# A bidirectional DeltaNet scan: state product on quarters, operands two steps ahead, a written order of two engines

## The chip, the cores and the metric

The kernel runs as one program on one core of a Trainium2 chip. The core has TensorE (PE, matmuls), VectorE (DVE), ScalarE (ACT), GpSimd (POOL) and SyncE (SP, which issues DMAs); each works through its own list of instructions in order, and semaphores hold an instruction until its inputs are there. The metric is the time of one execution on the device, in microseconds.

## The reference, cut to what matters

One layer of an encoder on 1024 tokens of width 1024: conditioning, a combined projection, two mixers side by side (attention and a gated DeltaNet), their gated merge, and a mixture of 16 experts. The DeltaNet runs forward and backward over 16 chunks of 64 tokens, 8 heads, 64 x 64 state each:

```python
T = triangular_solve(eye + L, eye)            # one 64x64 inverse per chunk, head, direction
def step(state, inp):
    u_n, w_n, a_n, qg_n, kd_n, gl_n = inp
    v_new = u_n - w_n @ state
    o_n = qg_n @ state + a_n @ v_new
    state = state * gl_n[..., None, None] + jnp.einsum('bhck,bhcv->bhkv', kd_n, v_new)
    return state, o_n
o = (o_fwd + o_bwd)
o = rmsnorm(o, dn_norm_w) * silu(dz)
mod = silu(c) @ W_ada + b_ada                  # six rows of 1024: the conditioning
```

The kernel computes all this in 32-bit floating point; a projection is three matmuls on high and low parts of its operands (hTh and hTl of the activations, wh and wl of the weights).

## The kernel before, in words

The stages follow each other: normalisation and the DeltaNet's projections with their short convolution (`dn_group`, to 210 us); decays and chunk products, two chunks at a time (`dn_tile`, to about 287); the inverse of 32 x 32 blocks on VectorE (`dn_invert`, lines 512 to 546, to 368.7), while TensorE does the attention's projections and the first gates (L285); the scan (`scan`, 399 to 707); attention, merge, output projection and experts.

The scan takes forward chunk t and backward chunk 15 - t in one step. Two chunks of 64 rows share the 128 partitions. `scan_load` brings a step's operands from DRAM on SP's queue. `scan_merge` makes the off-diagonal block of the two inverses from 32 x 32 blocks: VectorE transposes (L607), 16 small matmuls (L610), ScalarE, 16 more (L617), ScalarE. `scan_step` multiplies k and q by the state (L632): the state stands in `St` as block-diagonal 128 x 128 pairs of heads, which ScalarE copies anew from `Sc` each step (L665). Half of each product is the part for `X` = u - k state (L635, L639), the other half is the query's part of the output (L675 to L678). Then v_new (L644, L649, L650), the state's update (L654, L659, L662) and the output (L669).

Between these stand `fills`: matmuls of later projections (`late_fill`, L1154), each 128 x 512, 48 to a group; constants `FILL` say how many are asked for at which point of a step. In steps 0 to 7 `attn_prep` readies the attention's q, k and v for 128 tokens (transposes L149, VectorE L744 to L771), in later ones `scan_post` normalises finished output rows. `mods` works out the conditioning, a multiply-add on VectorE per 128 x 512 weight tile (L909), five groups of eight tiles before the scan, three in it; its sums go through a cast on ScalarE (L895), a difference on POOL (L896) and two matmuls (L898).

The order of instructions on each engine is set by a scheduler from the program's order and its own estimates, except within the inverse's columns, where VectorE's order is written down. Loads of the inverse's input run on POOL's queue.

```python
w = self.W[t % 2]                              # two sets of operands, loaded one step ahead
nc.tensor.matmul(pk[:, 2 * p:2 * p + 2, :].rearrange("p h c -> p (h c)"), kq[d][:, p],
                 self.St[:, d, p, :], start=True, stop=True, skip_group_check=True)   # L632
FILL = 12, 10, 8, 8, 48                        # per step 12 + 10 + 8 + 8, before the scan 48
```

## Time and profile before

| what | us |
|---|---|
| median of 3 runs | 1733.75 |
| lowest and highest | 1732.73, 1735.62 |
| the profiled execution, time | 1727.06 |
| its span in the trace | 1725.3 |
| TensorE busy | 1620.5 (94%) |
| VectorE busy | 1449.5 (84%) |
| ScalarE busy | 921.3 (53%) |
| mean granted clock of TensorE, share of full | 0.97 |

The profile shows one execution. Busy time of TensorE is modelled from pipelined matmuls that overlap, so the distance between starts tells more than the length of one. An fp32 matmul appears as two records, an fp32r one as one. A share of busy time is an average over stages with different limits; the rows below are therefore cut by stretches.

### The profile page before, as it was taken

Reading aid. Unit: us, or ns where it says so; the run is one execution under the profiler, and the core shown is the slowest. Engines: PE = TensorE matmul, PEld = TensorE weight load, DVE = VectorE, ACT = ScalarE, POOL = GpSimd, SP = SyncE. Lnnn points to the kernel's source line nnn. Section 1 sums busy time; section 2 is a strip of 40 time slices with the busy share of each in tenths; the row PEclk is TensorE's granted clock in tenths of the full one; section 3 lists DMA queues with packets and bytes.
Section 4 is the critical chain, followed back from the end, with each engine's and each line's share of the span. In section 5 each row is a group of like instructions: output and inputs, shape, how many; then the busy total and the mean of one; then the engine's idle time right before and its main releaser. Section 6 shows DMA issues by size and latency. Waiting matters only on the chain. (4 is left out here: it accounts for less than half of the span.)

```text
span 1725.3 us, 28697 instructions
## 1 busy us (share of the span) xinstructions
PE 1620.5 (94%) x10363; PEld 1291.2 (75%) x10363; DVE 1449.5 (84%) x2519; ACT 921.3 (53%) x1376; POOL 228.0 (13%) x223
## 2 busy tenths in 40 slices
PE   6999999789998999999999999669999999999997
PEld 4778777667776777778887788547777777777786
DVE  6799898966877779789986567979999999999996
ACT  6555432113433332588871323347777777777775
POOL 0010024021110000011112312300011000110000
PEclk8999999889998999999999999879999999999999
DMA  9466478247877885611136464769999999999981
GB/s 280 129 170 182 109 185 199 72 156 173 217 196 187 259 212 132 189 50 37 38 108 185 148 219 143 260 226 355 383 379 376 385 385 382 373 378 385 383 312 25
DMA packets 267597, 386.62 MB, mean 224 GB/s; under 512 B 62843, under 2 KB 136239, under 8 KB 266943
## 3 DMA queue, kind: packets, MB, share of 16 engines
q1 hardware_dynamic: 247615, 326.06, 57.2%
q0 software_dynamic: 13504, 47.19, 10.1%
q10 hardware_dynamic: 6336, 11.54, 1.8%
q8 instruction: 82, 1.34, 0.3%
q14 instruction: 60, 0.49, 0.1%
HBM read 326.99 MB, written 57.72 MB: 223 GB/s over the span
## 5 line engine op out<-in xcount | busy, mean ns | idle before, releaser
L1521 DVE TENSOR_TENSOR ew<-er,ew 128x1024 fp32r<-128x1024 f32 x384 | 452.4, 1220 | 29.2 <-ACT ew L1520 29.2
L1520 ACT CAST ew<-er 128x1024 fp32r<-128x1024 f32 x384 | 391.6, 1050 | 136.9 <-PE pj L1574 107.2
L1574 PE MATMUL pj<-ew,xT 128*128 128x512 f32 x1536 | 367.1, 396 | 4.5 <-DVE ew L1521 4.5
L1574 PEld LDWEIGHTS pj<-ew,xT 128*128 128x128 f32 x1536 | 282.8, 188 | 76.1 <-DVE ew L1521 19.5
L1591 PE MATMUL tr<-ew,aT 128*128 128x512 f32 x768 | 191.4, 398 | 0.0
L1591 PEld LDWEIGHTS tr<-ew,aT 128*128 128x128 f32 x768 | 139.7, 188 | 30.5 <-DVE ew L1521 3.5
L285 PE MATMUL pj<-hTh,wl 128*128 128x512 f32 (+1 forms) x368 | 118.9, 404 | 11.3 <-DVE wl L279 11.3
L285 PE MATMUL pj<-hTh,wh 128*128 128x512 f32 (+1 forms) x368 | 118.9, 402 | 3.5 <-ACT hTh L258 1.8
L285 PE MATMUL pj<-hTl,wh 128*128 128x512 f32 (+1 forms) x368 | 119.6, 402 | 1.4 <-DVE hTl L261 1.4
L278 ACT CAST wh<-wraw 128x1024 fp32r<-128x1024 f32 (+1 forms) x39 | 40.5, 1037 | 146.8 <-PE pj L285 110.9
L285 PEld LDWEIGHTS pj<-hTh,wl 128*128 128x128 f32 (+1 forms) x368 | 69.9, 191 | 28.9 <-DVE wl L279 12.1
L1597 POOL DMA_INDIRECT out_dram<-xe,idxT x16 | 37.3, 2328 | 410.2 <-DVE tok L1495 354.4
L840 DVE TENSOR_REDUCE am<-pj 128x1 f32<-128x1024 f32 x64 | 77.9, 1217 | 9.8 <-PE pj L835 9.3
L1200 PE MATMUL pj<-hTh,uw 128*128 128x512 f32 x256 | 83.5, 404 | 1.0 <-DVE uth L1206 0.5
L285 PEld LDWEIGHTS pj<-hTh,wh 128*128 128x128 f32 (+1 forms) x368 | 69.0, 190 | 19.4 <-ACT hTh L258 1.9
L1154 PE MATMUL pj<-hTh,wl 128*128 128x512 f32 x240 | 83.4, 415 | 0.0
L1154 PE MATMUL pj<-hTl,wh 128*128 128x512 f32 x240 | 83.0, 413 | 0.0
L1154 PE MATMUL pj<-hTh,wh 128*128 128x512 f32 x240 | 83.0, 411 | 0.0
L285 PEld LDWEIGHTS pj<-hTl,wh 128*128 128x128 f32 (+1 forms) x368 | 68.8, 189 | 17.6 <-DVE hTl L261 2.0
L275 POOL DMA_DIRECT2D wraw<-in_w_in_dram x36 | 32.6, 905 | 363.3 <-DVE wl L279 267.4
L842 ACT ACTIVATE ap<-pj,am 128x1024 f32<-128x1024 f32 x64 | 72.0, 1125 | 13.6 <-DVE am L840 7.4
L835 PE MATMUL pj<-kT,qT 128*128 128x512 f32 x256 | 74.5, 402 | 1.2 <-ACT ap L842 1.2
(380 smaller groups left out, 3029.9 us busy)
## 6 DMA issues: line engine op xcount, KB each, us to landing
er<-in_w_gate_dram SPq DMA_DIRECT2D x128, 512.0 KB
er<-in_w_up_dram SPq DMA_DIRECT2D x128, 512.0 KB
er<-in_w_down_dram SPq DMA_DIRECT2D x128, 512.0 KB
wraw<-in_w_in_dram POOLq DMA_DIRECT2D x36, 512.0 KB, 6.0
mw<-in_w_ada_dram SPq DMA_DIRECT2D x64, 256.0 KB
wt<-in_w_ada_dram SPq DMA_DIRECT2D x16, 512.0 KB
gate_d<-y ACTq DMA_DIRECT2D x32, 256.0 KB
kqs<-kq_d SPq DMA_DIRECT2D x32, 256.0 KB
```

Source lines behind the costliest of these rows:

```text
L278: nc.scalar.copy(wh[:, :, :n], raw[:, :, :n])
L285: self.nc.tensor.matmul(ps[q][:n], w[:, k, :n], x[k][:, q * 512:(q + 1) * 512], start=(k == 0 and w is wh and x is self.hTh), stop=(k == 7 ...
L835: nc.tensor.matmul(ps[:, kh], qT[:, i * 128:(i + 1) * 128], self.kT[a][:, s, kh * 512:(kh + 1) * 512], start=(s == 0), stop=(s == 1), skip ...
L840: nc.vector.reduce_max(m, ps, axis=AX.X, negate=True)
L842: nc.scalar.activation(p, ps, AF.Exp, bias=m, scale=1.0, accum_out=self.rv[:, h, half * 4 + i:half * 4 + i + 1])
L1154: nc.tensor.matmul(ps[q], a[:, k], x[k][:, q * 512:(q + 1) * 512], start=(k == 0 and a is wh and x is self.hTh), stop=(k == 7 and a is wl))
L1200: nc.tensor.matmul(ps, w[:, k], v[k][:, qs], start=(k == 0 and p == 0), stop=(k == 3 and p == 2))
L1520: nc.scalar.copy(hi, raw)
L1521: nc.vector.tensor_sub(lo, raw, hi.bitcast(F))
L1574: nc.tensor.matmul(pg[m], x[:, 2 * kp + k], wi[:, k], start=(kp == 0 and k == 0 and n == 0), stop=(kp == 3 and k == 1 and n == 2))
L1591: nc.tensor.matmul(py[q], x[:, k], wi[:, q], start=(k == 0 and n == 0), stop=(k == 7 and n == 2))
L1597: nc.gpsimd.indirect_dma_start(out=out2, out_offset=bass.IndirectOffsetOnAxis(ap=self.idx[:, e:e + 1], axis=0), in_=y, in_offset=None, com ...
```

## The change

1. State product: 32 matmuls of 64 x 64 on `Sc` itself in place of eight of 128 x 128 on `St`, which goes with its copies. The product is laid out so that one bank half holds `X`'s part and the other the output's, both on full 128 partitions; decays and norms are laid out to match (`egs`, `ssqs`), and an output is one addition (two from step 8).
2. Operands are loaded two steps ahead, in two parts. The transposed blocks are written to DRAM once after the inverse (ScalarE copies, `wt_d`) and loaded per step; L607 goes.
3. `attn_prep` comes in nine parts, `scan_post` in three; ScalarE empties the transposes' banks first. `slot` runs one part of everything pending, five times a step.
4. In the scan the order on TensorE and VectorE is the program's own (`manual_schedule`), and on VectorE in the whole inverse too.
5. Fills 8, 9, 9, 9 a step in place of 12, 10, 8, 8, and 60 before the scan in place of 48; six gate groups in place of five beside the inverse, so 14 late groups in place of 15. Their weights are split when half of the group before has been issued.
6. Conditioning: three groups before the inverse, five in steps 8 to 15 with four buffers; the sum is one fp32 matmul.
7. The inverse's input is loaded on SP's queue, the attention's operands on POOL's; projection weights beside `dn_tile` are fetched a group earlier.

```diff
--- before.py
+++ after.py
...
-INV = 8
-NGA = 5
+INV = 7
+NGA = 6
 QKV = 0, 2, 4
 DLY = 3
 MWB = 3
-MODG = 5
-MODS = 2, 2, 2
-FILL = 12, 10, 8, 8, 48
+MODG = 3
+MODS = 2
+FILL = 8, 9, 9, 9, 60
...
+    def raw_load(self, col):
+        raw = self.wp.tile([128, 8, 128], F, name="wraw", bufs=2)
+        self.nc.gpsimd.dma_start(raw, self.i["w_in"][0, :, col:col + 128].rearrange("(k p) c -> p k c", p=128))
+        return raw
+    def raw_split(self, raw):
+        wh = self.wp.tile([128, 8, 128], R, name="wh", bufs=2)
+        wl = self.wp.tile([128, 8, 128], R, name="wl", bufs=2)
+        self.nc.scalar.copy(wh, raw)
+        self.lo.tensor_sub(wl, raw, wh.bitcast(F))
+        return wh, wl
...
-            self.nc.gpsimd.dma_start(self.nb[d][16 * j0:16 * j1].rearrange("p b s c -> p (b s c)"),
-                                     self.nb_d[d, 16 * j0:16 * j1].rearrange("n b s c -> n (b s c)"))
+            self.nc.sync.dma_start(self.nb[d][16 * j0:16 * j1].rearrange("p b s c -> p (b s c)"),
...
             nc.sync.dma_start(self.w_d[d], ws[d].rearrange("p b s c -> p (b s c)"))
+            nc.scalar.copy(tmps[d][:, 0], ws[d][:, d].rearrange("p s c -> p c s"))
+            nc.scalar.dma_start(self.wt_d[d], tmps[d][:, 0].rearrange("p c s -> p (c s)"))
...
+            nc.sync.dma_start(self.wt[f], self.wt_d[d].rearrange("(n h) (c s) -> n c h s", h=8, s=32)[n])
...
+        yield w, at, kv, kq, nf, quads
...
-        for f, o, cf, co in quads:
-            nc.vector.transpose(wt[f], w[f, :, cf])
...
-        tmp = []
-        for d, n in enumerate(ns):
-            pk = self.pa.tile([128, 8, 64], F, name="dn", bufs=2)
+        tq = self.tq
+        pk = [self.pa.tile([128, 2, 4, 64], F, name="dn", bufs=2) for _ in range(2)]
+        for s, rows in enumerate((rs, os)):
             for p in range(4):
-                nc.tensor.matmul(pk[:, 2 * p:2 * p + 2, :].rearrange("p h c -> p (h c)"), kq[d][:, p],
-                                 self.St[:, d, p, :], start=True, stop=True, skip_group_check=True)
-            tp = self.tp[d]
-            nc.vector.tensor_mul(tp, pk, self.eg[:, n // 2, n % 2, d * 8:d * 8 + 8].unsqueeze(2)
-                                 .to_broadcast([128, 8, 64]))
-            tmp.append(tp)
-            r = rs[d]
-            nc.vector.tensor_sub(x[r], kv[r, 1].rearrange("p (h c) -> p h c", c=64), tp[r])
+                for d, hp in ((0, 0), (1, 1), (1, 0), (0, 1)):
+                    hr, r = slice(64 * hp, 64 * hp + 64), rows[d]
+                    nc.tensor.matmul(pk[hp][r, s, p], kq[d][hr, p, r], self.Sc[hr, d * 4 + p],
+                                     start=True, stop=True, skip_group_check=True)
+        for s, y in enumerate((x, tq)):
+            for hp in range(2):
+                nc.vector.tensor_mul(y[:, hp::2], pk[hp][:, s],
+                                     self.egs[:, s, t, hp::2].unsqueeze(2).to_broadcast([128, 4, 64]))
+            if s == 0:
+                nc.vector.tensor_sub(x, kv[:, 1].rearrange("p (h c) -> p h c", c=64), x)
+        ot = self.O(min(t, 15 - t))
+        if t > 7:
+            nc.vector.tensor_add(tq, tq, ot)
...
-                for hp in range(2):
-                    hr = slice(64 * hp, 64 * hp + 64)
-                    nc.scalar.copy(self.St[hr, d, :, hr], self.Sc[hr, d * 4:d * 4 + 4])
...
-        for d, n in enumerate(ns):
-            o = os[d]
-            ot = self.O(n // 2)[o].rearrange("p (h c) -> p h c", c=64)
-            if t < 8:
-                nc.vector.tensor_add(ot, tmp[d][o], po[o])
-            else:
-                nc.vector.tensor_add(ot, ot, tmp[d][o])
-                nc.vector.tensor_add(ot, ot, po[o])
-
-    def scan_post(self, j):
-
-        nc = self.nc
-        o = self.O(j).rearrange("p (h c) -> p h c", c=64)
+        nc.vector.tensor_add(ot, tq, po)
...
+        xq = wk.tile([128, 8, 64], F, name="xnq", bufs=1)
...
+        nc.scalar.copy(xq.rearrange("p h c -> p (h c)"), pq)
...
-        nc.sync.dma_start(self.kT[0].bitcast(F), self.kT_d[0:2].rearrange("h p t -> p h t"))
+        nc.gpsimd.dma_start(self.kT[0].bitcast(F), self.kT_d[0:2].rearrange("h p t -> p h t"))
...
+        for n in range(8 * g0, 8 * g1):
+            g, k = divmod(n, 8)
+            acc = self.macc[:, g % 2]
+            if k:
+                nc.vector.scalar_tensor_tensor(acc, self.mw[n % b], self.cs[:, k:k + 1], acc, op0=OP.mult, op1=OP.add)
+            else:
+                nc.vector.tensor_scalar(acc, self.mw[n % b], self.cs[:, 0:1], None, op0=OP.mult)
+            if k == 1 and done is not None:
+                self.mod_sum(done)
+            load(n + b)
+            if k == 7:
+                done = g
+            yield True
+        self.mod_sum(done)
...
-            hi, lo = (self.fp.tile([128, 512], R, name="y", bufs=2) for _ in range(2))
-            nc.scalar.copy(hi, acc)
-            nc.gpsimd.tensor_sub(lo, acc, hi.bitcast(F))
-            for s, t in enumerate((hi, lo)):
-                nc.tensor.matmul(ps[0:1], self.one, t, start=(s == 0), stop=(s == 1))
+            nc.tensor.matmul(ps[0:1], self.ones[:, 0:1], acc, start=True, stop=True)
...
+        def slot():
+            for g in behind[:]:
+                if next(g, 0) == 0:
+                    behind.remove(g)
...
+        with self.tc.manual_schedule(engines={ET.DVE, ET.PE}):
+            load = self.scan_load(0)
+            ops = next(load)
+            next(load)
+            behind.append(self.attn_prep(0, ak, self.pa))
+            slot()
+            fill(FILL[4])
+            for _ in self.scan_merge(ops):
+                fill(6)
+            load = self.scan_load(1)
+            nxt = next(load)
+            next(load)
+            for t in range(16):
+                step = self.scan_step(t, ops)
+                merge = self.scan_merge(nxt) if nxt else iter(())
+                load = self.scan_load(t + 2) if t < 14 else iter(())
+                next(step)
+                slot()
+                fill(FILL[0])
+                next(merge, None)
+                next(step)
+                ops, nxt = nxt, next(load, None)
+                slot()
+                fill(FILL[1])
+                next(step, None)
+                next(merge, None)
+                next(load, None)
+                if t > 7:
+                    behind.append(self.scan_post(15 - t))
+                slot()
+                fill(FILL[2])
+                slot()
+                fill(FILL[3])
+                if t < 7:
+                    behind.append(self.attn_prep(t + 1, ak, self.pa))
+                elif t == 7:
+                    behind.append(self.mods_late(MODG, 8))
+                slot()
+                if t == 8:
+                    sta.close()
+                    self.attn_load(self.pool(sta, "attn", side="right"))
...
+                with self.tc.manual_schedule(engines={mybir.EngineType.DVE}):
+                    for n, (f, c, g) in enumerate(fills):
+                        if n + 1 < len(fills):
+                            with self.tc.high_priority(offset=0):
+                                self.proj_ahead(fills[n + 1][1] + fills[n + 1][2] * 128)
+                        f(g)
+                        if n > 1:
+                            next(inv, None)
...
-                w = self.proj_load(late[n + 1][0] + late[n + 1][2] * 128)
+                raw = self.raw_load(late[n + 1][0] + late[n + 1][2] * 128)
...
+                if k == 4 and n + 1 < len(late):
+                    w = self.raw_split(raw)
```

VectorE in the inverse, before: nb and w are a block row's input and result of the two directions, wl the low part of the first gate group's weights (L279), with the columns around it.

```order
L535 TENSOR_TENSOR wtmp_2821<-nb_708,wb_2817 128x2x19x13
L535 TENSOR_TENSOR wtmp_2826<-nb_709,wb_2822 128x2x19x13
L539 TENSOR_TENSOR wb_2817<-wb_2817,wtmp_2821 128x2x19x13
L539 TENSOR_TENSOR wb_2822<-wb_2822,wtmp_2826 128x2x19x13
L279 TENSOR_TENSOR wl<-wraw,wh 128x1024
L535 TENSOR_TENSOR wtmp_2821<-nb_708,wb_2817 128x2x18x14
```

The same place after (L555 and L559 are the old L535 and L539):

```order
L555 TENSOR_TENSOR wtmp_2953<-nb_709,wb_2949 128x2x25x7
L555 TENSOR_TENSOR wtmp_2958<-nb_710,wb_2954 128x2x25x7
L559 TENSOR_TENSOR wb_2949<-wb_2949,wtmp_2953 128x2x25x7
L559 TENSOR_TENSOR wb_2954<-wb_2954,wtmp_2958 128x2x25x7
L279 TENSOR_TENSOR wl<-wraw,wh 128x1024
L555 TENSOR_TENSOR wtmp_2953<-nb_709,wb_2949 128x2x24x8
```

The split stood behind twelve columns of the inverse and stands behind seven. The operations of the conditioning, which stood between later columns, are gone from it.

TensorE in an early step, before, from the second half of the preparation's transposes (hl, kk and qraw are the attention's operands) over the state product (L632) to v_new (L644).

```order
L1154 MATMUL pj<-hTh_487,wl 128x512
L149 MATMUL tr<-masks,hl 128x128 x4
L1154 MATMUL pj<-hTh_528,wh 128x512
L632 MATMUL dn<-St,kqs 128x128 x2
L149 MATMUL tr<-masks,kk 128x128 x4
L632 MATMUL dn<-St,kqs 128x128 x2
L149 MATMUL tr<-masks,qraw 128x128 x6
L644 MATMUL dn<-st,W 64x64
L1154 MATMUL pj<-hTh_528,wh 128x512
L1154 MATMUL pj<-hTl_529,wh 128x512 x2
L1154 MATMUL pj<-hTh_528,wl 128x512
L644 MATMUL dn<-st,W 64x64 x15
```

TensorE in an early step after, from the state product (L654) to v_new (L669); L630 is the old L610, L1211 the old L1154.

```order
L654 MATMUL dn<-Sc,kqs 64x64 x32
L149 MATMUL tr<-masks,hl 128x128 x4
L149 MATMUL tr<-masks,qraw 128x128 x6
L1211 MATMUL pj<-hTh_652,wl 128x512 x2
L1211 MATMUL pj<-hTh_676,wh 128x512 x2
L1211 MATMUL pj<-hTl_677,wh 128x512 x2
L1211 MATMUL pj<-hTh_676,wl 128x512 x2
L630 MATMUL tr<-Sc 32x32 x16
L669 MATMUL dn<-st,W 64x64 x16
L149 MATMUL tr<-masks,hl 128x128 x4
```

The state product stood in two halves among the transposes, with v_new's first matmul directly behind it; it now stands in one piece, with ten transposes, eight fills and L630 between it and v_new.

VectorE in an early step, before, from the transpose of a block (L607) on: L635 and L639 make X, L649 and L650 scale v_new, L118 to L122 are a reciprocal root of the preparation.

```order
L607 STREAM_TRANSPOSE Sc<-W 32x256
L635 TENSOR_TENSOR st<-dn,eg 128x512
L639 TENSOR_TENSOR st<-kv,st 64x512
L744 TENSOR_REDUCE ass<-asq 128x10
L745 TENSOR_SCALAR ass<-ass 128x10
L118 TENSOR_SCALAR ra_y<-ass 128x10
L120 SCALAR_TENSOR_TENSOR ra_a<-ra_y 128x10
L649 TENSOR_TENSOR st<-dn,bs 128x512
L121 TENSOR_TENSOR ra_a<-ra_a,ass 128x10
L650 TENSOR_TENSOR st<-dn,bs 128x512
L122 SCALAR_TENSOR_TENSOR ra_y<-ra_a,ra_y 128x10
L662 TENSOR_TENSOR Sc<-st,dn 128x256
```

The same after: L658 and L661 make X and the output's part, L674 and L675 scale v_new, L767 and L771 are parts of the preparation.

```order
L658 TENSOR_TENSOR st<-dn,egs 128x4x64 x2
L661 TENSOR_TENSOR st<-kv,st 128x512
L658 TENSOR_TENSOR st<-dn,egs 128x4x64 x2
L767 TENSOR_TENSOR vst<-tr,vst 128x2x64
L674 TENSOR_TENSOR st<-dn,bs 128x512
L675 TENSOR_TENSOR st<-dn,bs 128x512
L771 TENSOR_REDUCE ass<-asq 128x10
L772 TENSOR_SCALAR ass<-ass 128x10
```

The two multiplications and the subtraction for X stand together now, the output's part behind them, and one part of the preparation stands in front of v_new.

## Rows read from the trace of the kernel before

**Rows 1.** Stretches: us; busy us (records) per engine; TensorE clock; DMA share; GB/s.

```profile
222.80:302.00 79.20, 76.13 (x727) 58.72 (x725) 69.91 (x140) 20.50 (x35) 28.41 (x46) 1.00 0.82 201
302.00:399.20 97.20, 79.36 (x346) 62.55 (x345) 73.87 (x150) 15.58 (x25) 13.35 (x10) 0.88 0.38 116
399.20:706.90 307.70, 295.88 (x3551) 234.92 (x3549) 241.49 (x551) 109.35 (x229) 29.72 (x45) 0.98 0.76 203
706.90:717.40 10.50, 10.50 (x55) 8.34 (x50) 9.19 (x29) 3.72 (x7) 0.00 (x0) 1.00 0.20 58
```

**Rows 2.** TensorE waits, 302 to 399: line, releaser, us, times, longest.

```profile
PE pj L285 <- DVE wl L279: 9.9, 1, 9.9
PE tr L898 <- ACT y L895: 4.0, 1, 4.0
```

**Rows 3.** Table by stretches: two stretches behind waits of TensorE.

```profile
325.40:331.00 5.60, 5.56 (x14) 4.41 (x15) 5.60 (x10) 0.00 (x0) 0.95 (x1) 0.52 0.33 94
382.00:389.00 7.00, 4.91 (x12) 3.35 (x13) 0.90 (x2) 0.62 (x1) 2.16 (x2) 0.51 0.42 145
```

**Rows 4.** Timeline, 368 to 394 us: start, us, engine, line, what [idle before].

```profile
368.66 0.82 SPq L545 DMA_DIRECT2D w_d<-wb  x2
...
387.44 0.84 SPq L588 DMA_DIRECT2D W<-w_d  x2
...
393.97 0.43 DVE L607 STREAM_TRANSPOSE Sc<-W 32x256 f32<-32x256 f32 x1 [6.27 <-DMA W<-w_d]
```

**Rows 5.** TensorE's waits in the scan, 399 to 707 us.

```profile
PE dn L644 <- DVE st L639: 4.5, 1, 4.5
```

**Rows 6.** Timeline of TensorE in one step of the scan.

```profile
472.18 0.68 PE L659 MATMUL dn<-st,kv 64*64 64x64 f32 x16
472.79 0.50 PE L1154 MATMUL pj<-hTh,wh 128*128 128x512 f32 x1
473.22 1.15 PE L669 MATMUL dn<-st,sa 64*64 64x64 f32 x32
474.30 0.74 PE L1154 MATMUL pj<-hTl,wh 128*128 128x512 f32 x2
474.88 0.63 PE L1154 MATMUL pj<-hTh,wl 128*128 128x512 f32 x2
475.34 0.62 PE L1154 MATMUL pj<-hTh,wh 128*128 128x512 f32 x2
...
476.59 0.69 PE L610 MATMUL tr<-Sc 32*32 32x32 f32 x32
477.21 1.16 PE L632 MATMUL dn<-St,kqs 128*128 128x128 f32 x8
478.13 0.47 PE L1154 MATMUL pj<-hTh,wl 128*128 128x512 f32 x1
```

**Rows 7.** Timeline of TensorE in dn_tile, the quarter products of k and q.

```profile
241.63 1.30 PE L477 MATMUL dn<-kq 64*64 64x64 f32 x64
242.87 0.74 PE L485 MATMUL tr<-rr,exc 128*128 128x512 f32 x2
```

**Rows 8.** Lines of TensorE in the scan: busy us, mean ns, idle before.

```profile
L1154 PE MATMUL pj<-hTh,wl 128*128 128x512 f32 x206 | 71.9, 415 | 0.0
```

**Rows 9.** Lines of VectorE in the scan, 399.2 to 706.9 us.

```profile
L635 DVE TENSOR_TENSOR st<-dn,eg 128x512 f32<-128x512 f32 x32 | 22.1, 689 | 17.4 <-PE dn L632 17.0
L639 DVE TENSOR_TENSOR st<-kv,st 64x512 f32<-64x512 f32 x32 | 21.9, 684 | 0.8
L909 DVE SCALAR_TENSOR_TENSOR macc<-mw,cs,macc 128x512 f32<-128x512 f32 x21 | 15.8, 753 | 8.9 <-DMA mw<-in_w_ada_dram 8.7
...
L607 DVE STREAM_TRANSPOSE Sc<-W 32x256 f32<-32x256 f32 x30 | 13.0, 434 | 0.7
L675 DVE TENSOR_TENSOR O<-st,dn 64x512 f32<-64x512 f32 x16 | 11.0, 685 | 2.3 <-PE dn L669 2.0
...
L662 DVE TENSOR_TENSOR Sc<-st,tr 128x256 f32<-128x256 f32 x15 | 6.3, 418 | 7.3 <-PE tr L659 6.9
```

More of the change, by code (lines that the diff above doesn't have):

```diff
@@ L402, in dn_gates @@
         nc.scalar.copy(flat[:, 1], e)
-        eg = self.ab.tile([128, NT, 2, 16], F, name="eg")
+        eg = sp.tile([128, NT, 2, 16], F, name="eg", tag="sq", bufs=1)
         gl = a.rearrange("p j (x e) -> p j x e", x=2)
@@ L431, in dn_gates @@
             nc.scalar.copy(gls[:, :, d * 4:d * 4 + 4], turn(gl[:, :, d * 4:d * 4 + 4]))
-        self.eg, self.gls, self.dk = eg, gls, dk
+        egs = self.ab.tile([128, 2, 16, 8], F, name="egs")
+        ev = eg.rearrange("p j x e -> p (j x) e")
+        for x in range(2):
+            for s in range(2):
+                lo, hi = (slice(64 * y, 64 * y + 64) for y in ((x + s) % 2, (1 - x + s) % 2))
+                nc.scalar.copy(egs[lo, s, x::2, :], ev[lo, x::2, 0:8])
+                nc.scalar.copy(egs[hi, s, x::2, :], rev1(ev[hi, 1 - x::2, 8:16]))
+        self.egs, self.gls, self.dk = egs, gls, dk
     def dn_scalars(self):
         nc, sp = self.nc, self.ap
-        nc.scalar.copy(self.ssqs[0:64], self.ssq[64:128])
-        nc.scalar.copy(self.ssqs[64:128], self.ssq[0:64])
+        for x in range(2):
+            here, there = slice(64 * x, 64 * x + 64), slice(64 - 64 * x, 128 - 64 * x)
+            nc.scalar.copy(self.ssqs[there, x::2], self.ssq[here, 0:4])
+            nc.scalar.copy(self.ssqs[there, 1 - x::2], rev1(self.ssq[here, 4:8]))
         rk2 = sp.tile([128, NT, 8], F, name="rk2", bufs=1)
@@ L580, in scan_load @@
         nf, at, kv = self.nf, self.sa[:, t % 2], self.kv[t % 2]
-        kq, quads = [], []
-        ns = (t, 15 - t)
+        quads, ns = [], (t, 15 - t)
+        kq = [self.kqs[d][:, t % 2] for d in range(2)]
         for d, n in enumerate(ns):
@@ L763, in attn_prep @@
         nc.scalar.copy(hl[:, :, 0].bitcast(R), rot)
+        yield
         nc.vector.tensor_sub(hl[:, :, 1], rot, hl[:, :, 0])
         kk = wk.tile([128, 2, 2, 2, 64], F, name="kk", bufs=1)
[L766 to L772 removed]
+        for c in range(2):
+            nc.scalar.copy(kk[:, :, :, c], hl[:, 8:10])
         for b in range(3):
@@ L878, in mods, with mod_place, mods_late, load @@
             yield True
+    def mod_place(self, g):
+        row, q = divmod(g, 2)
+        return row, slice(q * 512, (q + 1) * 512), 2 * D + row * D + q * 512
+    def mods_late(self, g0, g1):
+        nc, i = self.nc, self.i
+        done, b = None, len(self.mw)
+        def load(n):
+            if n < 8 * g1:
+                g, k = divmod(n, 8)
+                c0 = self.mod_place(g)[2]
+                nc.sync.dma_start(self.mw[n % b], i["w_ada"][0, k * 128:(k + 1) * 128, c0:c0 + 512])
+                if k == 5:
+                    nc.sync.dma_start(self.mb, i["b_ada"][:, c0:c0 + 512])
+        for n in range(8 * g0, 8 * g0 + b):
+            load(n)
+        yield True
+        for n in range(8 * g0, 8 * g1):
+            g, k = divmod(n, 8)
+            acc = self.macc[:, g % 2]
[8 more added lines that the diff above has]
+                done = g
+            yield True
+        self.mod_sum(done)
+    def mod_sum(self, g):
+        nc = self.nc
+        row, qs, _ = self.mod_place(g)
+        ps = self.pa.tile([128, 512], F, name="tr", bufs=2)
+        nc.tensor.matmul(ps[0:1], self.ones[:, 0:1], self.macc[:, g % 2], start=True, stop=True)
+        nc.vector.tensor_add(self.mb, self.mb, ps[0:1])
+        nc.sync.dma_start(self.mod_d[row:row + 1, qs], self.mb)
     def mod_step(self, n, g0, g1):
@@ L925, in fill @@
                 next(late, None)
-        def some(n):
-            for _ in range(n):
-                if behind:
-                    g = behind.pop(0)
-                    if next(g, 0) is None:
-                        behind.append(g)
-        def begin(g):
-            if next(g, 0) is None:
-                behind.append(g)
-        cur = iter(())
-        ops = self.scan_load(0)
-        prep = self.attn_prep(0, ak, self.pa)
-        next(prep)
-        fill(FILL[4])
-        for _ in self.scan_merge(ops):
-            fill(6)
@@ L982, in scan @@
             ps4.append(self.attn_scores(0, 0, i))
-            some(1)
         fill(10000)
-        while behind:
-            some(1)
         return ps4
@@ L1005, in mixer @@
             self.w_d = dnp.tile([2, 128, 2048], F, name="w_d")
+            self.wt_d = dnp.tile([2, 128, 1024], F, name="wt_d")
             self.qkv_d = dnp.tile([6, 128, S], F, name="qkv_d")
@@ L1080, in mixer @@
             t = self.unit("g17", (128, 2, 512), name="mw")
-            self.mod_tiles([t[:, n] for n in range(2)], self.unit("g18", (128, 2, 512), name="macc"))
-            self.more = self.mods(MODG, 8)
+            self.mod_tiles([t[:, 0], t[:, 1], self.mw2, self.mw3], self.unit("g18", (128, 2, 512), name="macc"))
             late = self.late_fill()
```

157 lines of the change are left out of this document (60 added, 97 removed).

## The prediction

> **What bounds the kernel now.** I read the table by stretches first [rows 1]. From 222.8 to 302 us and from 399.2 to 706.9 TensorE is busy 96% of the time; between 302 and 399.2, where VectorE inverts the blocks, TensorE is busy 79.4 of 97.2 us at a mean clock of 0.88. The scan is the longest stretch that the change touches: 307.7 us for 16 steps, TensorE 295.9, VectorE 241.5. From the merge on every engine keeps its instructions and their order, and the attention before it keeps its work, so what is won up to 717.4 moves all that follows one for one.
>
> Then the waits. In the stretch of the inverse TensorE waits 9.9 us for the low part of a projection's weights (L285 on VectorE's L279) and 4.0 us for the conditioning's cast [rows 2]; behind such waits it runs at about half of full clock, the lower of its two levels (granted 0.52 and 0.51, [rows 3]). The scan's start is held by operands, not by work: the inverse's result is issued to DRAM at 368.66, its reload only at 387.44, and VectorE's transpose of it starts at 393.97 after 6.27 us of waiting [rows 4]. In the scan one wait alone is 4.5 us [rows 5]. The named waits there are few; most of the stretch is work, so I count it.
>
> **Prices, from one step [rows 6].** Two fills (128x512 matmuls of a projection) start 0.46 us apart, so 0.23 each. Quarter matmuls: 32 records of L669 take 473.22 to 474.30, 1.08 us; 16 records of L659 take 0.61, so 1.22 for its 32. 32 records of 32x32 (L610) take 0.62. Eight 128x128 records (L632) take 0.92, 0.115 each, which I use for transposes of that size too. Two fills right after quarters take 0.58 in place of 0.46, so a change of the tile's size costs about 0.12.
>
> **The change, part by part.**
>
> *The product of the state.* Before, 16 records of 128x128 a step (1.84 us). After, 32 fp32 quarter matmuls, 64 records. The scan shows no such group; the nearest row is dn_tile's L477, 64 quarter records in 1.24 us [rows 7]. The other end is L669's pace, 64 x 1.08/32 = 2.16. I take 1.24, since both write rotating quarters. So between -0.6 and +0.3 us a step. The block-diagonal copy of the state and ScalarE's four copies of it vanish; they stood between the state and the product, and few waits name them.
>
> The rows above price a change of tile size at 0.12 us. The Trainium skill, TensorEngine Tiling (Array Packing), section Tiling Modes, says that a change of tiling mode drains TensorE, which speaks against this part: the old product ran in the mode of the fills around it, the new one does not. By the row it is two changes a step, about 4 us in 16 steps; were they free, the sum would be that much lower. The trace agrees that they are not free.
>
> *One step on TensorE after.* With a preparation (t under 8): 35 fills x 0.23 = 8.05; state product 1.24; L669 and L691 1.08 each; L684 1.22; L630 and L637 0.62 each; 18 transposes x 0.115 = 2.07; some eight changes of tile size x 0.12 = 0.96. Sum 16.9. Later steps: four transposes and a single matmul for the conditioning (0.46 + 0.25) in place of 2.07, sum 15.6. Sixteen steps: 8 x 16.9 + 8 x 15.6 = 260; the last one lacks L684 and a merge (2.5), and its last 18 fills (4.1) come behind the last output product: 253 up to there.
>
> Before, 618 fills stood in the 307.7 us (three operand pairs of about 206, [rows 8]); now 542. The 76 that left, 17 us, are found again in front and behind, below.
>
> *One step on VectorE.* It loses the full products' multiplications and half-height subtractions (L635 22.1, L639 21.9), the transposes (13.0) and the output's additions, L675 and two lines like it of 16 operations each (3 x 11.0): 90 us. It gains 64 multiplications of 128x256 x 0.418 = 26.8, 40 operations of 128x512 (16 subtractions, 24 additions) x 0.687 = 27.5, 16 more steps of the conditioning x 0.753 = 12.0 and two more output tails, four operations of 0.69 each, 5.5 [rows 9]. 241.5 - 90 + 71.8 = 223.3, or 14.0 a step: below TensorE's 15.6 to 16.9, but not by much.
>
> *Written order.* With operands two steps ahead, the waits that the trace names go. What is late next is VectorE's answer inside a step. After the state product TensorE has 10 transposes, 8 fills and L630 (1.15 + 1.84 + 0.62 = 3.6 us) before it needs X, for which VectorE does 2 x 0.418 + 0.687 = 1.5 us; before L684 it has 4 transposes and 9 fills (2.5 us) against one 0.69 us operation. The slack is there, but ScalarE's emptying of the transposes' banks sits in it too. No row shows a written order of this stage; bounds are 0 and, by TensorE's waits today, 4.5 us in a bad step. I allow 1 us a step, 16 us, which lies near the idle before L635 (17.4 us in 16 steps, [rows 9]). Scan: 253 + 16 = 269, or -39 us (0 to 35 us of waiting: -55 to -20).
>
> *Scan's start.* The 97.2 us from 302 hold 346 records of TensorE [rows 1], all but some 38 small ones fills: about 308 x 0.23 + 1.5 = 72 us of work. 25 are lost, 14 of them in the waits of [rows 2], most of the rest at half clock. After, the weights' split stands between the inverse's parts and the conditioning is gone from here. But by TensorE's list 45 more fills stand between dn_tile's start (222.8) and the first state product (one more gate group, 60 fills in place of 48 in front of the scan, less what the earlier fetch lets go ahead of dn_tile): 10.3 us, and the first late fill needs a split that stands behind the inverse, which I put at 5 us of waiting. -25 + 10.3 + 5 makes -10. The other path agrees: the inverse's end near 370 (368.7 now, with one more split in it), copies about 2 (two of 128x1024), write and reload about as W's landing now, 6 each, a first merge of two groups with a copy after each, 2 to 4: 386 to 390. So first product at 389 instead of 399.2; bounds -16 (no wait at all) and 0 (the load chain as long as now). Loading on the queues moves with it: the blocks' reload goes from POOL to SP, where it stands behind nothing long; the attention's loads go the other way and land before they are used.
>
> *Tail.* Behind the last output product 18 + 46 fills and all 16 first score matmuls of the attention (of the fills' shape) remain, 80 x 0.23 = 18.4 us, against 10.5 before, where half of the scores and more of the fills had gone ahead of it [rows 1]: +8.
>
> *Sum.* -10 - 39 + 8 = -41. The profiled execution took 1727.06 us, so 1686; the median of the runs shown is 6.7 above that execution: 1693. Own range 1677 to 1709.
>
> **Rivals.**
>
> *The start gains nothing* (more fills stand in dn_tile, and two more DRAM transfers lie behind the inverse). For: reload took 25 us from write to use [rows 4]. Against: that was the queue standing behind the conditioning. 1703.
>
> *Quarters at L669's pace*: +0.92 x 16 = 15, so 1708. For: same fp32 64x64 form as L669. Against: L477 [rows 7].
>
> *Late conditioning starves VectorE.* All of five groups' 40 operations now fall in eight steps, and in a fixed order one that waits for its 256 KB holds the state's operations behind it. Before, 21 of them waited 8.9 us in all, 0.42 each; 40 x 0.42 = 17: 1710. Against: four buffers instead of two.
>
> *Written order locks both engines (slower).* Place: VectorE's preparation parts and output tail, which stand in front of the state's operations of the next step. One part late delays X, then L669, L684 and the state, with no fill allowed to pass. It becomes slower than before from 41 + 16 = 57 us of waiting, 3.6 us a step; at 4 us a step it is 64 - 16 = 48 more: 1741. For: VectorE idles 66 us of today's scan (307.7 - 241.5), and is filled to about 85% of a step after. Against: the slack counted above. The wait of 9.9 us [rows 2] shows how one late operation in VectorE's order holds TensorE. The Trainium skill, TensorE: Matmul & The Clock Gate, section on the array's architectural detail, says that VectorE's queue is strictly first in, first out; the trace agrees, and by that rule this rival's time is the one just given.
>
> **How the numbers follow.** Forecast 0.61 (1693), start 0.10 (1703), conditioning 0.10 (1710), quarters 0.06 (1708), locked 0.13 (1741). The range is 1669 to 1722: below it no waiting at all and the full gain at the start would be needed; its upper end takes in two of the milder rivals together. 0.2% (3.5 us) is about what can be told from no change. The locked case gives 0.10 slower and 0.03 the same; the others 0.86 faster and 0.01 the same: faster 0.86, same 0.04, slower 0.10.
>
> **What would show it.** First state product (L654) near 389. State product's 64 records in about 1.3 us. L691 to L691 about 17.5 us in the first half and 16.5 in the second, 269 us in all; TensorE's waits on VectorE inside a step about 1 us, none on DMA. VectorE about 223 us busy in the scan. No half-clock stretch near 325 or 540. The forecast is wrong if steps stay near 19 us, if the first product comes at 399 or later, or if VectorE's waits name the conditioning's loads.

## The result and the profile after

The changed kernel takes 1746.09 us (median of 5; 1741.56 to 1747.63) where the kernel before, run beside it, takes 1732.73: ratio 1.007, 95% interval 1.0053 to 1.0087. 41 us less were forecast; it is 13 more. The profiled execution has a span of 1739.7 us against 1725.3, so its 14.4 us can be laid out by stretches.

First the table by stretches of the changed kernel (columns as in [rows 1]), cut at its own first state product (392.8) and the end of its last output product (710.6):

```profile
302.00:392.80 90.80, 79.15 (x386) 64.06 (x384) 64.58 (x135) 19.38 (x25) 7.17 (x8) 0.93 0.43 132
392.80:710.60 317.80, 255.13 (x4214) 202.42 (x4210) 220.16 (x535) 87.84 (x190) 21.11 (x31) 0.92 0.78 206
710.60:732.00 21.40, 20.47 (x94) 15.37 (x89) 13.35 (x26) 8.32 (x14) 3.28 (x3) 1.00 0.59 182
```

The scan starts 6.4 us earlier (399.2 before), lasts 317.8 instead of 307.7, and its tail 21.4 instead of 10.5: -6.4 + 10.1 + 10.9 = +14.6. In the scan TensorE works 255 us instead of 296 and VectorE 220 instead of 241 [rows 1]: the work went down as forecast, and the stretch grew. TensorE idles 62.7 of the 317.8 us. The mean granted clock fell from 0.98 to 0.92; as in [rows 3], half clock comes behind a wait in the step shown below. TensorE's waits in the scan (engine, line, releaser: us, times, longest):

```profile
PE dn L669 <- DVE st L658: 17.5, 4, 9.3
PE tr L149 <- DVE hl L795: 13.2, 8, 3.5
PE tr L149 <- DVE st L714: 9.6, 7, 2.3
PE dn L669 <- issue: 7.5, 2, 4.3
PE tr L149 <- DMA qraw<-qkv_d: 6.0, 2, 4.1
PE tr L149 <- DVE Sc L687: 5.0, 5, 1.0
```

59 us stand in these rows; before, the longest was a single 4.5 [rows 5]. Most are of two kinds. L669 (v_new) waits for X (its two `issue` waits too: each ends 0.4 us after L661 has made X), and the transposes L149 wait for what stands right before them on VectorE. VectorE's lines, from 392.8 to 709.6 us (busy, mean | idle before and its releaser), tell where X is held:

```profile
L658 DVE TENSOR_TENSOR st<-dn,egs 128x256 f32<-128x256 f32 x64 | 23.9, 416 | 11.3 <-PE dn L654 11.3
...
L661 DVE TENSOR_TENSOR st<-kv,st 128x512 f32<-128x512 f32 x16 | 11.3, 709 | 0.5
...
L720 DVE SCALAR_TENSOR_TENSOR dz<-tr,colt,dz 128x512 f32<-128x512 f32 x7 | 5.3, 751 | 32.6 <-DMA dz<-dz_d 28.0 <-DMA Sc<-wt_d 4.5 <-PE tr L149 0.2
```

L720, the output tail's last operation, idles 32.6 us, 28.0 of them put down to its dz rows, in five steps. It stands in front of the next step's L658. The worst step (timeline: start, us, engine, line; SPq is SP's queue of transfers):

```profile
590.52 1.02 PEld L654 LDWEIGHTS dn<-Sc,kqs 64*64 64x64 f32 x64 [0.17 <-DMA st<-in_w_ada_dram]
...
591.61 0.73 PE L1211 MATMUL pj<-hTl,wh 128*128 128x512 f32 x2
...
592.25 1.90 SPq L703 DMA_DIRECT2D dz<-dz_d  x2
...
593.65 0.58 PEld L630 LDWEIGHTS tr<-Sc 32*32 32x32 f32 x32 [0.35 <-issue]
...
600.98 0.75 DVE L720 SCALAR_TENSOR_TENSOR dz<-tr,colt,dz 128x512 f32<-128x512 f32 x1 [8.79 <-DMA dz<-dz_d]
601.65 0.75 DVE L658 TENSOR_TENSOR st<-dn,egs 128x256 f32<-128x256 f32 x2
...
602.43 0.69 DVE L661 TENSOR_TENSOR st<-kv,st 128x512 f32<-128x512 f32 x1
...
603.61 1.97 PE L669 MATMUL dn<-st,W 64*64 64x64 f32 x32 [9.26 <-DVE st L658]
```

The state product is done at 591.61. dz is issued by SP from 592.25 on, L720 starts at 600.98, only behind it X is made (L658, L661), and L669 starts at 603.61 after 9.26 us. From there to 606 the granted clock is 0.50, the lower of its two levels (table by stretches, changed kernel):

```profile
603.60:606.00 2.40, 2.40 (x33) 2.28 (x34) 1.93 (x4) 0.00 (x0) 0.00 (x0) 0.50 0.31 68
```

dz lands late for two reasons. SP issues it late, because in SP's list it stands behind SP's stores and the conditioning's loads (SP's queue, steps 8 to 15, first two of its waits; the first is partly dz's own doing, since L722 stores what L720 makes):

```profile
SPq L722 <- DVE st L658: 20.0, 6, 5.1
SPq L919 <- DVE macc L930: 12.8, 10, 2.7
```

And the load itself takes a median of 6.7 us from issue to landing, where the trace tells it, among the other transfers (DMA issues, 560 to 710 us: count, KB, median us):

```profile
dz<-dz_d SPq DMA_DIRECT2D x16, 128.0 KB, 6.7
```

In early steps the second kind of wait rules. hl's low part (L795) ends at 518.2 and the transposes that use it stand directly behind the state product:

```profile
515.52 1.16 PE L654 MATMUL dn<-Sc,kqs 64*64 64x64 f32 x64
...
517.36 0.82 DVE L795 TENSOR_TENSOR hl<-asq,hl 128x640 f32<-128x640 f32 x1 [0.85 <-ACT hl L793]
...
518.33 0.63 PE L149 MATMUL tr<-masks,hl 128*128 128x128 f32 x4 [1.65 <-DVE hl L795]
```

### The profile page after: what moved, and what is told of

Same layout as the page of the kernel before. It is cut to its first block, busy times and chain, and to the rows that moved or that the text cites. A ratio compares the mean times of both kernels' runs of the same rounds, so it can differ in the third digit from the quotient of the medians.

```text
span 1739.7 us, 30181 instructions
## 1 busy us (share of the span) xinstructions
PE 1593.5 (92%) x11131; PEld 1270.9 (73%) x11131; DVE 1416.4 (81%) x2470; ACT 907.1 (52%) x1352; POOL 208.3 (12%) x196
## 5 line engine op out<-in xcount | busy, mean ns | idle before, releaser
L1648 PEld LDWEIGHTS tr<-ew,aT 128*128 128x128 f32 x768 | 139.7, 188 | 30.4 <-DVE ew L1578 3.4
L297 PE MATMUL pj<-hTh,wl 128*128 128x512 f32 (+1 forms) x384 | 123.4, 399 | 6.3 <-DVE wl L279 6.3
L297 PEld LDWEIGHTS pj<-hTh,wl 128*128 128x128 f32 (+1 forms) x384 | 71.8, 188 | 23.6 <-DVE wl L279 6.8
L1211 PE MATMUL pj<-hTh,wl 128*128 128x512 f32 x224 | 77.4, 422 | 0.0
L1211 PE MATMUL pj<-hTh,wh 128*128 128x512 f32 x224 | 76.4, 419 | 0.0
L1211 PE MATMUL pj<-hTl,wh 128*128 128x512 f32 x224 | 76.4, 418 | 0.0
L278 ACT CAST wh<-wraw 128x1024 fp32r<-128x1024 f32 (+1 forms) x26 | 26.7, 1028 | 87.7 <-PE pj L297 87.7
L325 DVE SCALAR_TENSOR_TENSOR y<-xc,colt,y 128x1024 f32<-128x1024 f32 x48 | 61.3, 1278 | 1.5 <-ACT y L323 1.0
```

The source lines that it names most:

```text
L297: self.nc.tensor.matmul(ps[q][:n], w[:, k, :n], x[k][:, q * 512:(q + 1) * 512], start=(k == 0 and w is wh and x is self.hTh), stop=(k == 7 ...
L325: nc.vector.scalar_tensor_tensor(y, xc[:, t:t + S], w(t), y, op0=OP.mult, op1=OP.add)
L1211: nc.tensor.matmul(ps[q], a[:, k], x[k][:, q * 512:(q + 1) * 512], start=(k == 0 and a is wh and x is self.hTh), stop=(k == 7 and a is wl))
L1648: nc.tensor.matmul(py[q], x[:, k], wi[:, q], start=(k == 0 and n == 0), stop=(k == 7 and n == 2))
```

## The experiments

Three theories from these rows. **A, places:** instructions that wait for a load or another engine stand in the written order in front of the state's operations or without work before them. **B, queue:** SP's queue, where stores that wait for engines and the conditioning's loads stand in front of operands, brings everything late. **C:** a written order as such costs.

Ratios are to runs of the kernel before on the same chip. That kernel's median was between 1729.7 and 1733.4 us in these comparisons, and the changed kernel did not run beside the others, so medians of different chips do not show a few us. "Won" therefore compares ratios: the changed kernel's 1.0070 minus the run's, times 1733 us, with both intervals combined. "First" and "last" are starts of the output product of steps 0 and 15 in the profiled execution, and the longest step is the time from one such start to the next, named by the step that ends it; changed kernel: 404.2, 709.6, 27.3. The runs that change nothing before step 8 (e1, e3, e5, e6) have their first output product anywhere from 404.5 to 409.3, so "first" tells little by itself.

| run | median us | ratio, 95% interval | won, us | first, last | longest step, t > 7 |
|---|---|---|---|---|---|
| e1 dz ahead | 1732.9 | 1.0024 (1.0005 to 1.0043) | 8 ± 4 | 404.5, 701.6 | 26.4 |
| e2 fills first | 1750.3 | 1.0125 (1.0101 to 1.0149) | -10 ± 5 | 409.6, 718.2 | 30.7 |
| e3 conditioning off SP | 1730.9 | 1.0010 (0.9994 to 1.0027) | 10 ± 4 | 408.2, 697.4 | 24.2 |
| e4 free order | 1730.2 | 0.9999 (0.9982 to 1.0016) | 12 ± 4 | 407.4, 712.8 | 29.0 |
| e5 tail late | 1733.3 | 1.0022 (1.0010 to 1.0033) | 8 ± 4 | 408.6, 704.2 | 28.6 |
| e6 = e1 + e3 | 1725.0 | 0.9974 (0.9958 to 0.9991) | 17 ± 4 | 409.3, 693.4 | 26.4 |
| e7 stores off SP | 1742.7 | 1.0081 (1.0060 to 1.0101) | -2 ± 5 | 407.1, 711.1 | 31.9 |
| e8 all | 1705.5 | 0.9856 (0.9838 to 0.9873) | 37 ± 4 | 408.1, 680.4 | 23.8 |
| e9 free, queues | 1726.7 | 0.9976 (0.9951 to 1.0000) | 16 ± 5 | 412.1, 696.4 | 28.4 |
| e10 = e8, loads spread | 1709.3 | 0.9864 (0.9846 to 0.9882) | 36 ± 4 | 408.2, 678.7 | 30.9 |
| e11 queues only | 1725.1 | 0.9953 (0.9938 to 0.9969) | 20 ± 4 | 406.4, 692.2 | 27.2 |
| e12 = e8, gate stores | 1703.3 | 0.9822 (0.9780 to 0.9863) | 43 ± 8 | 408.5, 678.1 | 29.6 |
| e13 = e12, qraw | 1693.0 | 0.9756 (0.9716 to 0.9797) | 54 ± 8 | 406.0, 669.2 | 30.4 |
| e14 = e13, loads spread | 1689.9 | 0.9747 (0.9719 to 0.9775) | 56 ± 6 | 407.9, 670.4 | 20.9 |
| e15 = e14, free order | 1700.8 | 0.9828 (0.9793 to 0.9863) | 42 ± 7 | 407.0, 664.7 | 20.7 |

**e1.** The load of dz moves to the end of the tail before (two of its edits):

```diff
-            nc.sync.dma_start(zt[:, :, 64 * b:64 * b + 64], ...)    # at the start of scan_post(m)
+        if m:
+            self.post_load(m - 1)                                   # behind L720
```

> The changed kernel, with the output tail's dz rows loaded one step ahead (right after the tail of the step before has read the buffer) instead of at the start of the tail that uses them. Theory A (place in the written order): VectorE's L720 stands in front of the next step's state operations and waits 32.5 us in all for that load, TensorE's L669 waits 25 us behind it. Then L720's waits fall under 5 us, steps 8 to 15 fall from about 20.7 to about 17.5 us, total 20 to 30 us less than the changed kernel's 1746, about 1720. Theory B (SP's queue too full with the conditioning's loads): other loads are late in its place, the waits of L669 move to the conditioning's or the operands' loads, gain under 8 us.

8 us won, not 20 to 30. L720 now waits 1.3 us and L669 0.4, as A says; but the waits behind it grew, as B says (TensorE's waits in e1's scan; L717 is the changed kernel's L714):

```profile
PE tr L149 <- DVE st L717: 14.6, 7, 3.7
PE tr L149 <- DVE hl L800: 14.6, 8, 3.5
PE tr L630 <- DMA Sc<-wt_d: 12.2, 4, 7.6
```

**e2.** In each step `fill(...)` goes in front of `slot()` (the first of its places):

```diff
-                slot()
                 fill(FILL[0])
                 next(merge, None)
+                slot()
```

> The changed kernel, with each step's fills put in front of the pending parts (and so of their transposes) instead of behind them; VectorE's and ScalarE's work is the same. Theory A': TensorE's transposes stand right behind the VectorE operation whose result they need (hl 13.2 us, st 10.5, kk about 8 in the scan); with 6 to 9 fills between, 20 us of these waits go and steps 0 to 7 fall from about 19.5 to 18 us: total about 1727. Theory B (SP's queue) expects no change in the first half's waits on DMA (6 us) and under 5 us in all. A third: waits only move to L669 and L684, whose slack was those fills: no gain or a loss.

Its third case: the waits on hl fall from 13.2 to 3.9 us, but VectorE's L767, which stands in front of v_new's scaling, now waits 28.6 us for ScalarE instead of 13.7. From the first output product to the last it takes 308.6 us instead of 305.4. By the ratios 10 us are lost.

**e3.** `nc.sync` becomes `nc.gpsimd` for the conditioning's weight tiles in `mods_late`.

> The changed kernel, with the conditioning's 40 weight tiles of the scan loaded on GpSimd's queue instead of SyncE's. Theory B: SP's queue, which waits 20 us before the output stores and 20 us before these loads in steps 8 to 15, is what brings dz and the operands late; with 5 issues a step gone, dz lands 3 to 5 us earlier, L720's waits fall from 32.5 to about 10 us, total about 1725. Theory A: the dz load is still issued within the step that uses it, behind the same stores: L720's waits stay above 20 us, gain under 10 us.

B's numbers for the waits: L720 waits 8.5 us instead of 32.5, though SP still stands 28 us in front of the tail's stores. In the step that was the worst dz is now issued at 576.51 instead of 592.25, and L720 does not wait (timeline, e3):

```profile
576.51 1.02 SPq L703 DMA_DIRECT2D dz<-dz_d  x2
...
596.04 0.73 DVE L720 SCALAR_TENSOR_TENSOR dz<-tr,colt,dz 128x512 f32<-128x512 f32 x1
```

So dz was issued late because of the loads before it on SP. Won are 10 us, half of what B expected.

**e4.** `with ExitStack():` in place of the scan's `manual_schedule`.

> The changed kernel without the written order in the scan: the scheduler sets the order of TensorE and VectorE there as in the kernel before; everything else of the change stays. Theory C (the written order as such costs): the scan falls below the kernel before's 307 us, towards 275 to 285, total about 1710 to 1720. Theory A: the scheduler also puts the pieces late or early by its estimates; the gain is what its order avoids of L720's 32 us and the transposes' 29 us, so between 1715 and 1740. If the quarter product, the parts or the late conditioning cost by themselves, it stays at 1740 or above.

In total the scheduler's order wins about what e1 or e3 win, and C's 1710 to 1720 is not reached. But it wins it in another way: TensorE idles 23.6 us in the scan instead of 62.7, and L720 waits for no dz. The scan is no shorter for it (305.4 us from first to last output product in both), because 638 matmuls of 128x512, of projections and of the attention's scores, stand in it instead of 542. Of its three long steps only the second waits, 7.2 us for the blocks' loads; the others are nearly full of work (table by stretches of e4: the scan, then the steps t = 2, 11 and 12):

```profile
393.20:712.80 319.60, 296.00 (x4307) 226.35 (x4306) 218.45 (x539) 99.66 (x210) 18.60 (x30) 0.94 0.77 202
424.70:452.30 27.60, 26.66 (x318) 21.12 (x319) 15.67 (x39) 9.36 (x19) 2.68 (x4) 1.00 0.51 126
596.60:625.60 29.00, 21.85 (x283) 16.49 (x282) 13.71 (x34) 4.25 (x8) 0.90 (x1) 0.88 0.83 232
625.60:650.40 24.80, 24.64 (x299) 18.06 (x298) 16.09 (x36) 4.25 (x8) 0.00 (x0) 1.00 0.66 166
```

So this run alone does not decide on C; e9 and e15 do.

**e5.** One `yield` more in `scan_post` in front of the transposes.

> The changed kernel, with the last part of the output tail (transposes of st, L720 and its store) one turn later: VectorE's L720 now stands behind the next step's X instead of in front of it; load, queues and everything else are as changed. Theory A (its place in VectorE's order): L669's 25 us of waiting on VectorE fall under 8, the transposes' 10.5 us on L714 under 3, total 20 to 25 us less than 1746, about 1723. Theory B (SP's queue): loads stay late, L720 then holds L674 and TensorE waits at L684 instead: gain under 10 us.

8 us, within what B expected. L669's waits are gone, and the same late dz now holds the next operation in VectorE's order, L674, as B put it. VectorE's wait in e5's scan, and TensorE's for what it held:

```profile
DVE dz L721 <- DMA dz<-dz_d: 25.6, 6, 7.7
```

```profile
PE dn L684 <- DVE st L674: 16.7, 5, 4.9
```

**e6.** e1 and e3 together.

> The changed kernel with dz one step ahead and the conditioning's tiles on GpSimd's queue, which won 13 and 15 us alone. If both took away the same wait (L720 on dz), together they give no more than one: about 1730. If the queue holds more than dz (the blocks' loads nf and wt, 12.2 us of TensorE's waits with dz ahead alone), they add up: 1715 to 1722.

1725.0, between the two cases. By the ratios the gains add up (17 against 8 and 10); in the profiles they do so only in part (from first to last output product 297.1 in e1, 289.2 in e3, 284.1 in e6, against 305.4).

**e7.** `qT_d`, `kT_d` stores on ScalarE's queue, `vS_d` and `dn_d` on GpSimd's.

> The changed kernel, with the stores of the preparation and of the output tail on ScalarE's and GpSimd's queues, so that SP's queue in the scan has loads, and the conditioning's small store, only. SP waits 15.5 us for ScalarE's qst, 7.5 us for vst in the first half and 20 us for L720's result in the second, with loads behind. Theory B: operands and dz then come early; L720's waits fall under 15 us, L630's and qraw's waits on DMA (11 us) under 4, total 1720 to 1728. Theory A: the dz load still starts in its own step, 1738 or more.

L720 still waits 26.5 us, and the ratio shows no gain. The stores alone were not what held dz; A's case for this run.

**e8.** e1, e3, e5, e7, one `yield` more in `attn_prep` in front of the transposes of hl, and the two norms' loads on GpSimd's queue.

> The changed kernel with all of it: dz one step ahead, the conditioning's tiles on GpSimd's queue, stores off SP, the output tail's and the preparation's last parts one turn later, and the query and key norms' loads on GpSimd's queue, so that the scan's first loads need not stand behind them. If places and queue are the whole loss: the scan at about 280 us instead of 305, its start 4 us earlier, total 1712 to 1718, below the kernel before. If VectorE's own chain of about 17.5 us a step bounds it (13.4 us busy and the answers of ScalarE and TensorE in it), 1720 to 1727.

1705.5, 1.4% under the kernel before, and under the expected range by 6 us. Its start did not come 4 us earlier (first output product at 408.1, against 404.2). **e11** takes the two extra `yield` out again:

> The version with all mended, but with the output tail's and the preparation's last parts back in their old turn: only the queues are mended. Theory A (places on top of queues): the transposes' waits on hl and st (13.2 and 11.8 us with dz ahead and the conditioning's tiles moved) come back, 1718 to 1725. Theory B (the queue alone): 1708 or less.

1725.1: TensorE's waits on hl and st are back in the scan (13.0 and 12.6 us), and with the same queues the two places are worth 17 us by the ratios. **e9** has e11's queues and a free order:

> The changed kernel without the written order in the scan and with the queues mended (dz one step ahead, the conditioning's tiles, the stores and the two norms' loads off SP). With the free order alone it took 1730 and TensorE waited 13.4 us there for the blocks' loads, three steps of 25 to 29 us. If those were SP's queue: about 1712 to 1718. If a written order with its places mended (1705.5) is worth something by itself, this stays 5 us or more above that; if the order is worth nothing, it is 1706 or less.

1726.7, not 1712 to 1718, with steps of 35 and 28 us. Queues alone bring either order to 1725 to 1727, so the written order as such costs nothing that these runs can tell, and C falls; A and B are both needed.

**e10.** The attention's five loads one a step, by `yield` between them.

> The version with all mended (1705.5), with the attention's five loads (3.5 MB) spread over steps 8 to 12, one a step, instead of issued together after step 8. Every kernel so far has its longest step of the second half there (22 to 32 us; 23.8 and 22.6 in this version, others about 15.5). If that burst is the cause, these two steps fall to about 17 and the total to 1693 to 1697; if it is the conditioning's own chain on GpSimd's queue, the gain is under 4 us.

No gain from the spreading by itself. The long step is still there, and ScalarE stands in it (its waits, 570 to 612 us):

```profile
ACT W L639 <- DMA Sc<-n_d: 15.4, 1, 15.4
```

Its order has a gate's store directly ahead, and that store waits on a semaphore on which SP's operand loads count too: L639 itself does not read what the named load, `Sc<-n_d`, brings. **e12** moves the store:

```diff
-                (nc.sync if c == C_DZ else nc.scalar).dma_start(dst[g, :, q * 512:(q + 1) * 512], th)
+                (nc.sync if c == C_DZ else nc.gpsimd).dma_start(dst[g, :, q * 512:(q + 1) * 512], th)
```

> The version with all mended (1705.5), with the gates' stores in the scan (gate_d) issued on GpSimd's queue instead of ScalarE's. In the version with the attention's loads spread ScalarE stood 15.4 us before one L639, behind such a store that waited for an earlier load's end, and VectorE and TensorE behind it: the one step of 24 to 31 us. If that is the long step of every version, the longest step from t=8 on falls under 18 us and the total to 1692 to 1697. If the burst of loads after step 8 makes it by itself, a step over 22 us stays and the total is above 1702.

Its second case: ScalarE's wait is gone, and a step of 29.6 us stays. VectorE waits there for a tile of the conditioning, and TensorE's L630 behind it for the bank of the conditioning's sum, which VectorE empties (L953). Waits of VectorE and of TensorE in e12's scan:

```profile
DVE macc L937 <- DMA mw<-in_w_ada_dram: 11.6, 1, 11.6
```

```profile
PE tr L630 <- DVE mb L953: 12.0, 2, 10.8
PE tr L149 <- DMA qraw<-qkv_d: 11.7, 1, 11.7
```

**e13.** The last of these rows, the wait at t = 1: qraw and rp on GpSimd's queue as well. In e12 SP issues that qraw only at 420.1, behind the operands for two steps on; in front of one of these loads SP stood 3.5 us, until an earlier operand had landed (SP's waits, 395 to 445 us):

```profile
SPq L610 <- DMA kqs<-kq_d: 3.5, 1, 3.5
```

> The same, with the preparation's loads (qraw, rp) on GpSimd's queue too. On SP's queue they stand behind the operands two steps ahead, whose buffers come free only when the step in progress has used them; TensorE's transposes waited 9.5 to 10.9 us for qraw in the second step (27 us). If that order makes the long second step, it falls to about 19 and the total by another 6 to 9 us against the run beside it; if the step is long by other first loads, it stays over 24 and the totals agree within 3 us.

1693.0. This qraw is now issued at 400.1, step t = 1 falls from 29.1 to 19.9 us, and the wait on qraw is gone. So operands "two steps ahead" delay what stands behind them. With two sets of buffers the load for step t + 2 can moreover start only when step t has used its set, and SP waits for that (changed kernel, SP's waits, 404 to 560 us; L618 loads kqs, L654 reads it):

```profile
SPq L618 <- PE dn L654: 6.5, 3, 2.7
```

A third set wasn't tried.

**e14.** e13 with e10's spreading.

> The version of 1693.0 with the attention's loads spread over steps 8 to 12 as well. Its one long step left (30.4 us, t = 10) has TensorE's L630 12 us behind VectorE, which waits 12.5 us for a tile of the conditioning that stands behind the attention's 3.5 MB on GpSimd's queue. If the burst makes that wait, the step falls to about 17 us and the total to 1680 to 1684; if the tile is late by something else, a step over 22 us stays and the total is above 1689.

The step at t = 10 falls from 30.4 to 19.6 us, so the burst on the conditioning's queue made most of that wait; but t = 11 and t = 14 rose (14.3 to 20.6, 14.6 to 20.9; why is open), and the total, 1689.9, agrees with e13 within the intervals. The expected 1680 to 1684 wasn't reached.

**e15.** e14 without the written order.

> The same kernel as the one beside it (all queues mended, attention's loads spread, parts one turn later), without the written order of TensorE and VectorE in the scan. If the written order is worth something once nothing stands in its way, this is 5 us or more slower than the version beside it. If the scheduler's order is as good, within 5 us; if a written order costs by itself, it is the faster of the two.

By the medians, on one chip, the written order earns 11 us, and the intervals lie apart; but the profiled executions do not show it (span 1691.6 free, 1693.5 written). The free one was the fastest of its runs (1693.4), the written one the slowest (1695.5). What the order earns is not located.

## Why the prediction was wrong

**The step that failed** is "Written order", where I put 16 us of waiting ("I allow 1 us a step"). The sum of work there was 253 us up to the last output product; measured are 316.8 from the first state product to its start, so about 64 us of waiting (TensorE idles 62.7), four times the allowance, above the 35 of the term's own bounds, and beyond the 57 from which the fourth rival, "Written order locks both engines", decides. That rival named the place ("preparation parts and output tail, which stand in front of the state's operations") and gave 1741 against the measured 1746; I gave it 0.13. It was put aside by a slack that counted the state's own operations and TensorE's fills, and not L720 in front of X, nor the transposes without a fill before them.

**"With operands two steps ahead, the waits that the trace names go"** failed with it. No row of before could show the new order's waits, but the new code showed that a load two steps ahead needs the buffer of the step in progress, and that SP's list has the conditioning's loads, and stores that wait for VectorE and ScalarE, between the operands. e13 prices what stands behind the operands at 10 us, e3 the conditioning's loads at 10, and for the stores alone e7 shows nothing.

**The conditioning rival** had the right load and the wrong form: in the changed kernel VectorE waits for dz behind those loads on SP (e3), and for the tiles themselves only once they stand behind the attention's loads on another queue (e12: 11.6 us).

**The product of the state** was right: 64 records in 590.52 to 591.61, 1.09 us (forecast 1.24; before 1.84).

**The steps' work** came out right in sum, in part by luck. e13's steps t = 5 to 8 take 17.0, 16.8, 16.6 and 16.0 us (sum 16.9 for a step with preparation), and its last ones 14.6 and 15.3 (15.6). But TensorE still idles 1.0 to 1.3 us in each of the four, and the state's update (L684) took 0.52 us where the sum has 1.22. VectorE is busy 220 us (223).

**The start** came at 392.8, not 389, inside its bounds: TensorE's L630 waited 4 us for the blocks' transposed loads. They stood on SP behind the norms' loads, but e8 takes those off SP and starts no earlier, so that this was the reason is not shown.

**The tail** was +10.9 instead of +8; 1 us of it waits for the last output rows (L714).

**The clock** was left out of the sum: the scan's mean of 0.92 instead of 0.98 comes with the waits, as in [rows 3]; its share of the loss is not separated here.

With most of the waits mended, e13 comes to 1693.0, the time forecast. That is no merit of the forecast: it needed eight edits more (e8's six, e12, e13).

## What to carry to other kernels

Before an order is written down for two engines, list for each instruction on the recurrence everything that stands in front of it on its engine, and ask of each of those which load or engine it waits for; here slack counted along the recurrence alone missed 64 us. In an operand ring of two buffers the load for step t + 2 waits until step t has used its buffer, whatever the call says, and what stands behind it on the queue waits too: look in the trace at what the queue itself waits for. Queue and place have to be mended together; by the ratios the tail's place alone (e5) won 8 us here, the queues alone (e11) 20, and both (e8) 37.

## What the runs showed of the hardware

The state's update, 32 records of 64 x 64 that go round all four quarters of the array and two banks, took 0.52 us from its first start to the start of what follows, in the changed kernel's timeline; 16 records on two quarters into one bank took 0.61 before [rows 6]. Whether the quarters or the banks make the difference no run separates.

```profile
526.24 0.27 PE L684 MATMUL dn<-st,kv 64*64 64x64 f32 x1
...
526.76 0.45 PE L691 MATMUL dn<-st,sa 64*64 64x64 f32 x9
```

ScalarE's copies with turned axes took 2.1 us for 128x1024 (4.18 for two), where its cast of the same size, with the axes in order, took 1.05 a few us later:

```profile
364.87 4.18 ACT L566 COPY wtmp<-wb 128x1024 f32<-128x1024 f32 x2 [4.48 <-DVE wb L559]
...
372.06 1.05 ACT L290 CAST wh<-wraw 128x1024 fp32r<-128x1024 f32 x1 [1.29 <-issue]
```

An engine that issues a store stood still with all its work until that store could start: ScalarE 15.4 us in e10.
